# Attention with a bias on one NeuronCore: groups that go on with the last chunks, places filled as they come free, and a rearranged start

## The chip, the cores and the metric

The kernel runs on one core of a Trainium2 chip. A core has five engines that run side by side and wait for one another through semaphores: TensorE (PE; its weight loads are listed apart as PEld), VectorE (DVE), ScalarE (ACT), GpSimd (POOL) and SyncE (SP). SP, ACT and POOL also issue DMA transfers. The metric is the device time of one execution in microseconds; lower is better. The time before is 250.87 us, the median of three runs (250.59 to 251.34).

## The reference

Four batches of eight heads, 1024 positions, head size 64, all float32; the bias is one 1024 x 1024 matrix for all heads:

```python
scores = scale * np.matmul(q, k.transpose(0, 1, 3, 2))     # scale = 1/8
scores = scores + bias
scores_max = np.max(scores, axis=-1, keepdims=True)
attn = np.exp(scores - scores_max) / (np.sum(np.exp(scores - scores_max), axis=-1, keepdims=True) + 1e-8)
return np.matmul(attn, v).astype(np.float32)
```

The kernel works in bfloat16, leaves the maximum out (the values are small), and gets the sum of the exponentials from a column of ones beside v.

## The kernel before

**Slots.** The 32 heads are taken as 16 pairs; a pair's q and k lie side by side as 128 columns. The 1024 queries of a head are 8 chunks of 128. One chunk of one head is a slot, so there are 256 slots. A slot's scores (128 x 1024) are made in one of three *places* in PSUM (`places`), by 8 matmuls of 128 x 128 (`fill`, L210). ACT takes the exponential of a place in one instruction (`exp`, L217) and writes an E tile (9 buffers, `NE`). PE then multiplies E with v (`av`, L276, 8 matmuls) into a bank shared with the transposes (`ps_x`, two tags, xa and xb). When a batch of six slots is done, VectorE divides by the sums (`evac`, L284 and L287), and SP sends the rows out (L300).

**The bias is put into a place once.** The first fill of a place for a chunk adds the bias by 8 more matmuls against a scaled identity (L205). After that, the next head's fill goes on top: its operands hold the next head's product and, with the sign turned, the last head's, so that one matmul takes the old scores out and puts the new ones in. That is what the doubled operands are for: `ko`, `qo` for odd heads, `ke`, `qe` for even ones, where one half of `ke` and `qe` comes from the pair before (`double`, L183 and L185; part 1 writes into the next pair's arrays). A slot with a bias fill uses `qe` of the first pair, or `qs` of a pair in the middle, whose lower half is zero. `linked` says whether a pair's arrays go on into the next pair; it is false at the end of a group.

**Groups.** The pairs fall into three groups of 4, 6 and 6. Within a group the chunks go 0 to 2 for all heads (place x takes chunk x), then 3 to 5, and then 6 and 7, where the third place takes chunks 6 and 7 of the last third of the heads. Every group starts all of it anew, so there are 30 bias fills.

**VectorE does some exponentials.** 15 slots, spread evenly over batches (`dslots`), have no exponential on ACT: VectorE makes it in seven instructions (`d_steps`, L237 to L260), the first of which (`dy`) frees the place.

**Preparing q and k.** Each pair is loaded by POOL's DMA queue with a cast (L128, L129), copied side by side by VectorE (`side_by_side`, L135), transposed by PE (L165, 8 per piece), copied out of PSUM by VectorE (`copy_out`, L172 and L174), and doubled, on VectorE if it is wanted soon, else on POOL. v goes straight into its array (L146), or, for the first four pairs, through a landing tile and a VectorE copy (L414). Pair 0's q and k and the first bias row come as float32 by the queues of SP and ACT and are cast by VectorE and ACT (L305 to L341).

**The order of the work** is written out by a planner that runs when the kernel is built. It keeps a clock for each engine with assumed costs in ns (a fill 450, `AV` 255, an exponential 906, a ke copy 340), and emits at each step the instruction that can start first. Slots are filled strictly in their order (`next_fill`); transposes of a piece are emitted in one go. Each engine then runs its list in that order, and waits where an operand isn't ready.

Of the kernel before, what the change touches and what calls it, by code (L numbers as in the profile page):

```python
# [16 lines left out]
def kernel(  # L17
# [13 lines left out]
    nc = tc.nc  # L31
# [23 lines left out]
    qsp = ctx.enter_context(tc.tile_pool(name="qsp", bufs=1))  # L55
    ep = ctx.enter_context(tc.tile_pool(name="ep", bufs=NE))
    op = ctx.enter_context(tc.tile_pool(name="op", bufs=3))
# [10 lines left out]
    sgn = consts.tile([P, 1], F32)  # L68
    zeros = consts.tile([P, 512], BF)
# [3 lines left out]
    q0f = consts.tile([P, 2, NCH, D], F32)  # L73
# [3 lines left out]

    slots = []
    batches = []
    first_pair, split_pair = set(), set()  # L80
    group_of = {}
    pr0 = 0
    for g, n in enumerate(GROUPS):
        heads = list(range(2 * pr0, 2 * (pr0 + n)))
        for pr in range(pr0, pr0 + n):
            group_of[pr] = g
        first_pair.add(pr0)
        rounds = []
        for c in (0, 3):
            rounds += [[(x, c + x, h, h == heads[0]) for x in range(3)] for h in heads]  # L90
        a = (len(heads) * 2 // 3 + 1) // 2 * 2
        tail = [(2, c, h, h == heads[a]) for c in (6, 7) for h in heads[a:]]
        split_pair.add(heads[a] // 2)
        for i, h in enumerate(heads[:a]):
            rounds.append([(0, 6, h, h == heads[0]), (1, 7, h, h == heads[0])] + tail[i:i + 1])
        assert len(tail) <= a
        for i in range(0, len(rounds), 2):
            b = []
            for r in rounds[i:i + 2]:
                b += range(len(slots), len(slots) + len(r))  # L100
                slots += r
            batches.append(b)
        pr0 += n
    NS, NB = len(slots), len(batches)
# [14 lines left out]
    can = [b for b in range(2, NB - 3) if len(batches[b]) == 6]  # L119
    ND = 15  # L120
    dslots = [batches[can[(2 * i + 1) * len(can) // (2 * ND)]][5] for i in range(ND)]
    aslots = [s for s in range(NS) if s not in dslots]
# [3 lines left out]
    def load_qk(pr):  # L126
        f = [land.tile([P, 2, NCH, D], BF, name=x) for x in ("q16", "k16")]
        nc.gpsimd.dma_start(out=f[1].rearrange("p t c d -> p t (c d)"), in_=kf[pr])  # L128
        nc.gpsimd.dma_start(out=f[0].rearrange("p t c d -> p t (c d)"), in_=qf[pr])  # L129
        lands[pr] = f  # L130

    def side_by_side(pr, x):

        t = raw.tile([P, NCH, 2, D], BF, name="qk"[x] + "r")
        nc.vector.tensor_copy(t.rearrange("p c t d -> p t c d"), lands[pr][x][:])  # L135
        raws[pr, x] = t
# [11 lines left out]
    def arrays(pr):  # L148
        if pr not in arrs:
            t = {x: kq.tile([P, NCH, P], BF, name=x) for x in ("ko", "ke", "qo", "qe")}  # L150
            if pr in split_pair:
                t["qs"] = qsp.tile([P, NCH, P], BF, name="qs")
                nc.gpsimd.memset(t["qs"][D:, :, :], 0.0)
            if pr in first_pair:
                (nc.gpsimd if pr else nc.vector).memset(t["qe"][D:, :, :], 0.0)
            arrs[pr] = t
        return arrs[pr]

    def linked(pr):
        return pr + 1 < NP and pr + 1 not in first_pair  # L160

    def transposes(pr, which, c0, n, tag):
        px = ps_x.tile([P, n, P], BF, tag=tag, name="px")
        for c in range(n):
            nc.tensor.transpose(px[:, c, :], raws[pr, which][:, c0 + c].rearrange("p t d -> p (t d)"), ident[:])  # L165
        return px
# [9 lines left out]
    def double(pr, which, c0, n, part, w):  # L176
# [7 lines left out]
        else:  # L184
            w.tensor_scalar(to["qs" if part == 2 else "qe"][rows, cs, :], t["qo"][rows, cs, :], -1.0, 1.0,  # L185
                            op0=ALU.mult, op1=ALU.mult)

    def parts(pr, which):
        return ([0] if not which or pr not in first_pair else []) + ([1] if linked(pr) else []) + (
            [2] if not which and pr in split_pair else [])  # L190

    def operands(s):
# [3 lines left out]
        if start:  # L196
            return t["ko"], t["qe"] if pr in first_pair else t["qs"]
        return (t["ko"], t["qo"]) if h % 2 else (t["ke"], t["qe"])

    def fill(s):  # L200
        x, c, h, start = slots[s]
        ps = places[x]
        if start:
            for kc in range(NCH):
                nc.tensor.matmul(ps[:, kc // 4, kc % 4 * P:(kc % 4 + 1) * P],  # L205
                                 braw[:, c, :].rearrange("p (kp kc) -> p kc kp", kc=NCH)[:, kc, :], ident8[:],
                                 start=kc % 4 == 0, stop=False, skip_group_check=True)
        kk, qq = operands(s)
        for kc in range(NCH):
            nc.tensor.matmul(ps[:, kc // 4, kc % 4 * P:(kc % 4 + 1) * P], kk[:, kc, :], qq[:, c, :],  # L210
                             start=False, stop=True, skip_group_check=True)
# [3 lines left out]
    def exp(s):  # L215
        etile[s] = ep.tile([P, NCH, P], BF, name="E")
        nc.scalar.activation(etile[s].rearrange("p c q -> p (c q)"), places[slots[s][0]].rearrange("p b x -> p (b x)"),  # L217
                             ACTF.Exp, scale=scale)
# [60 lines left out]
    def evac(b):  # L279
# [7 lines left out]
        nc.vector.tensor_tensor(ob[:, :m, :], po[:, :m, :D], rs[:, :m, :].to_broadcast([P, m, D]), op=ALU.mult)  # L287
# [15 lines left out]
    with tc.manual_schedule():  # L303

        nc.sync.dma_start(out=k0f[:, 0].rearrange("p c d -> p (c d)"), in_=kf[0][:, 0])  # L305
        nc.scalar.dma_start(out=q0f[:, :, :C0].rearrange("p t c d -> p t (c d)"), in_=qf[0][:, :, :C0 * D])
        nc.sync.dma_start(out=k0f[:, 1].rearrange("p c d -> p (c d)"), in_=kf[0][:, 1])
        nc.scalar.dma_start(out=b0f[:], in_=bf_[:, 0, :])
        nc.sync.dma_start(out=q0f[:, :, C0:].rearrange("p t c d -> p t (c d)"), in_=qf[0][:, :, C0 * D:])
# [6 lines left out]
        nc.gpsimd.dma_start(out=braw[:, 1, :], in_=bf_[:, 1, :])  # L316
        nc.gpsimd.dma_start(out=braw[:, 2, :], in_=bf_[:, 2, :])
        load_qk(1)
        for i in range(10):
            nc.tensor.matmul(places[2][:, 0, :], zeros[:, :P], zeros[:], start=True, stop=True)  # L320
        qr0 = raws[0, 0] = raw.tile([P, NCH, 2, D], BF, name="qr")
        kr0 = raws[0, 1] = raw.tile([P, NCH, 2, D], BF, name="kr")
        t0 = arrays(0)
        nc.vector.memset(vall[:, :, :, D:D1], 1.0)
        nc.vector.tensor_scalar(ident8[:], ident[:], 1.0 / scale, None, op0=ALU.mult)
        load_v(0)
        load_qk(2)
        load_v(1)
        load_qk(3)
        load_v(2)  # L330
        nc.vector.tensor_copy(qr0[:, :C0].rearrange("p c t d -> p t c d"), q0f[:, :, :C0])
        nc.vector.tensor_copy(kr0[:, :, 0, :], k0f[:, 0])
        nc.vector.tensor_copy(kr0[:, :, 1, :], k0f[:, 1])
        nc.scalar.copy(braw[:, 0, :], b0f[:])  # L334
        pq = transposes(0, 0, 0, C0, "xa")
        for i in range(2):
            nc.tensor.matmul(places[2][:, 0, :], zeros[:, :P], zeros[:], start=True, stop=True)
        copy_out(0, 0, 0, C0, pq)
        nc.vector.tensor_copy(t0["qe"][:D, :C0, :], pq[:D])
        copy_out(0, 1, 0, NCH, transposes(0, 1, 0, NCH, "xb"))  # L340
# [357 lines left out]
```

## Time and profile before

| | |
|---|---|
| median of three runs | 250.87 us |
| profiled execution, its time | 251.34 us |
| its span | 249.57 us |
| exponentials on ACT | 241 (224.0 us busy) |
| first exponential starts, last one ends | 10.69 us, 244.16 us |
| seventh exponential (the first of pair 1) starts | 17.87 us |
| VectorE busy | 203.0 us |
| PE busy | 227.8 us |
| bias fills | 30 (240 matmuls of L205) |

The span begins with the first instruction of the program and ends with its last. "Busy" is the time in which an engine has at least one instruction running; instructions overlap at their ends, so the mean duration of one may be more than busy time over their number. PE clock stays at full speed from 4.7 us to the end of the work. The page names a wait by what ended it.

### The profile page before, as it was taken

Reading aid. Unit: us, or ns where it says so; the run is one execution under the profiler, and the core shown is the slowest. Engines: PE = TensorE matmul, PEld = TensorE weight load, DVE = VectorE, ACT = ScalarE, POOL = GpSimd, SP = SyncE. Lnnn points to the kernel's source line nnn. Section 1 sums busy time; section 2 is a strip of 40 time slices with the busy share of each in tenths; the row PEclk is TensorE's granted clock in tenths of the full one; section 3 lists DMA queues with packets and bytes.
Section 4 is the critical chain, followed back from the end, with each engine's and each line's share of the span. In section 5 each row is a group of like instructions: output and inputs, shape, how many; then the busy total and the mean of one; then the engine's idle time right before and its main releaser. Section 6 shows DMA issues by size and latency. Waiting matters only on the chain.

```text
span 249.6 us, 10411 instructions
## 1 busy us (share of the span) xinstructions
PE 227.8 (91%) x4604; PEld 216.3 (87%) x4604; DVE 203.0 (81%) x334; ACT 226.5 (91%) x244; POOL 69.5 (28%) x86
## 2 busy tenths in 40 slices
PE   8579999999999989998897999898999999999981
PEld 3469999899999989998897999898999998899970
DVE  5389788897969999999999999999999773977111
ACT  2479999999997999999998999899999999999991
POOL 8335986171461413535740002300000000000000
PEclk9999999999999999999999999999999999999997
DMA  6999999996987699799592021101111111111121
GB/s 214 223 205 209 207 206 189 202 128 92 139 131 61 105 123 133 123 129 131 96 96 67 3 68 37 34 24 51 43 53 34 39 58 30 41 34 46 29 65 33
DMA packets 53229, 24.53 MB, mean 98 GB/s; under 512 B 31680, under 2 KB 51904, under 8 KB 53184
## 3 DMA queue, kind: packets, MB, share of 16 engines
q0 software_dynamic: 35216, 13.90, 47.8%
q1 hardware_dynamic: 17552, 9.25, 13.3%
q8 instruction: 36, 0.59, 1.0%
q10 hardware_dynamic: 416, 0.72, 0.9%
q14 instruction: 9, 0.07, 0.1%
HBM read 29.36 MB, written 8.39 MB: 151 GB/s over the span
## 4 chain that ended last, share of the span: by engine, by line
PE 47%; DVE 23%; ACT 12%; issue 11%; DMA 4%; ACTq 1%; SPq 0%; DVEq 0%
PE pl L210 26%; PE po L276 13%; ACT E L217 11%; PE pl L205 6%; DVE dy L237 3%; DMA b0f<-in_bias_dram 3%; PE px L165 3%; DVE ob L287 3%; DVE ke L183 2%; DVE qo L174 2%; DVE ko L172 1%; DVE qe L185 1%; DVE de L260 1%; DVE dpw L246 1%; DVE rs L284 1%
## 5 line engine op out<-in xcount | busy, mean ns | idle before, releaser
L217 ACT ACTIVATE E<-pl 128x1024 bf16<-128x1024 f32 x241 | 224.0, 1079 | 10.7 <-PE pl L210 8.5
L276 PE MATMUL po<-vall,E 128*128 128x65 bf16 x1928 | 93.9, 194 | 3.4 <-DVE qo L174 1.9
L276 PEld LDWEIGHTS <-E 128*128 128x128 bf16 x1928 | 79.3, 98 | 4.6 <-issue 2.4
L210 PEld LDWEIGHTS <-ko 128*128 128x128 bf16 x1264 | 75.8, 98 | 3.3 <-issue 0.7
L210 PE MATMUL pl<-qo,ko 128*128 128x128 bf16 x1024 | 76.3, 219 | 1.3 <-issue 0.6
L210 PE MATMUL pl<-qe,ke 128*128 128x128 bf16 x784 | 58.5, 219 | 4.6 <-DVE dy L237 3.2
L210 PEld LDWEIGHTS <-ke 128*128 128x128 bf16 x784 | 47.1, 98 | 7.7 <-issue 4.2
L284 DVE RECIPROCAL rs<-po 128x6 f32<-128x6 f32 (+2 forms) x43 | 8.3, 193 | 23.4 <-PE po L276 23.1
L287 DVE TENSOR_TENSOR ob<-po,rs 128x384 f32<-128x384 f32 (+2 forms) x43 | 22.9, 531 | 1.8 <-DVE rs L284 0.3
L205 PE MATMUL pl<-ident,braw 128*128 128x128 bf16 x240 | 19.9, 226 | 4.1 <-ACT braw L334 3.0
L146 POOL DMA_DIRECT2D vall<-in_v_dram x24 | 22.3, 934 | 1.4 <-DMA vall<-in_v_dram 1.2
L205 PEld LDWEIGHTS <-braw 128*128 128x128 bf16 x240 | 18.1, 148 | 4.7 <-ACT braw L334 3.2
L237 DVE TENSOR_SCALAR dy<-pl 128x1024 int32<-128x1024 f32 x15 | 18.3, 1220 | 3.7 <-PE pl L210 3.3
L185 POOL TENSOR_SCALAR qe<-qo 64x1024 bf16<-64x1024 bf16 (+1 forms) x10 | 12.6, 1261 | 30.5 <-DVE qo L174 30.0
L128 POOL DMA_DIRECT2D k<-in_k_dram x15 | 11.0, 731 | 36.1 <-DVE kr L135 32.5
L249 DVE SCALAR_TENSOR_TENSOR dy<-df 128x1024 f32<-128x1024 f32 x15 | 19.0, 1269 | 0.3
L256 DVE SCALAR_TENSOR_TENSOR db<-db,dpw 128x1024 f32<-128x1024 f32 x15 | 18.3, 1221 | 0.3
L260 DVE SCALAR_TENSOR_TENSOR de<-dy,db 128x1024 bf16<-128x1024 f32 x15 | 18.3, 1220 | 0.2
L249 DVE SCALAR_TENSOR_TENSOR db<-df 128x1024 f32<-128x1024 f32 x15 | 18.2, 1217 | 0.0
L183 DVE COPY ke<-ko 64x1024 bf16<-64x1024 bf16 x26 | 15.4, 594 | 0.7
L129 POOL DMA_DIRECT2D q<-in_q_dram x15 | 11.5, 768 | 12.7 <-DVE qr L135 11.0
L210 PE MATMUL pl<-qe,ko 128*128 128x128 bf16 x192 | 14.6, 219 | 0.0
(49 smaller groups left out, 149.2 us busy)
## 6 DMA issues: line engine op xcount, KB each, us to landing
out_dram<-ob SPq DMA_DIRECT2D x52, 96.0 KB, 2.7
k<-in_k_dram POOLq DMA_DIRECT2D x15, 256.0 KB, 4.9
q<-in_q_dram POOLq DMA_DIRECT2D x15, 256.0 KB, 7.2
vall<-in_v_dram POOLq DMA_DIRECT2D x24, 128.0 KB, 6.7
out_dram<-ob SPq DMA_DIRECT2D x34, 64.0 KB, 1.7
braw<-in_bias_dram POOLq DMA_DIRECT2D x7, 256.0 KB, 7.8
v<-in_v_dram POOLq DMA_DIRECT2D x4, 256.0 KB, 8.1
out_dram<-ob SPq DMA_DIRECT2D x17, 32.0 KB, 1.6
```

The lines of the kernel that those rows point to most:

```text
L146: nc.gpsimd.dma_start(out=vall[:, 2 * pr + t, :, :D], in_=vf[pr, :, t])
L183: w.tensor_copy(to["ke"][rows, cs, :], t["ko"][rows, cs, :])
L185: w.tensor_scalar(to["qs" if part == 2 else "qe"][rows, cs, :], t["qo"][rows, cs, :], -1.0, 1.0, op0=ALU.mult, op1=ALU.mult)
L205: nc.tensor.matmul(ps[:, kc // 4, kc % 4 * P:(kc % 4 + 1) * P], braw[:, c, :].rearrange("p (kp kc) -> p kc kp", kc=NCH)[:, kc, :], ident8[ ...
L210: nc.tensor.matmul(ps[:, kc // 4, kc % 4 * P:(kc % 4 + 1) * P], kk[:, kc, :], qq[:, c, :], start=False, stop=True, skip_group_check=True)
L217: nc.scalar.activation(etile[s].rearrange("p c q -> p (c q)"), places[slots[s][0]].rearrange("p b x -> p (b x)"), ACTF.Exp, scale=scale)
L237: w.tensor_scalar(y[:], places[slots[s][0]].rearrange("p b x -> p (b x)"), scale * LOG2E * 65536.0, 127.0 * 65536.0, op0=ALU.mult, op1=ALU ...
L249: w.scalar_tensor_tensor(o[:], t["f"][:], c, t["f"][:], op0=ALU.add, op1=ALU.mult)
L256: w.scalar_tensor_tensor(t["b"][:], t["b"][:], V2, t["p"].bitcast(BF), op0=ALU.add, op1=ALU.mult)
L260: w.scalar_tensor_tensor(etile[s].rearrange("p c q -> p (c q)"), t["a"], V1, t["b"][:], op0=ALU.add, op1=ALU.mult)
L276: nc.tensor.matmul(po[:, j, :], etile[s][:, kc, :], vall[:, h, kc, :], start=j == 0 and kc == 0, stop=kc == NCH - 1, skip_group_check=True)
L287: nc.vector.tensor_tensor(ob[:, :m, :], po[:, :m, :D], rs[:, :m, :].to_broadcast([P, m, D]), op=ALU.mult)
```

## The change

- *Groups go on with the last chunks.* A group's chunks are now three stretches: three chunks at one end, chunks 3 and 4 in the middle (third place: chunks 3 and 4 of the last third of the heads), and three chunks at the other end. Odd groups run from chunk 5 down to 0, so that a group begins with the chunks with which the one before ended and needs no new bias there. `linked` now holds for all pairs but the last. Bias fills: 24. The last round's three slots are a batch of their own.
- *Places filled in order of release.* Each place has its own queue of slots, and the planner may fill any place whose next slot is at most 4 (`WINDOW`) beyond the oldest open one. Which slots VectorE takes is decided while planning: a slot of place 2 goes to VectorE if its backlog is under 5000 ns (`ROOM`). There are 16 of them.
- *Half transposes.* A piece's transposes are emitted in two halves, other work may stand between them, and they are held back while E tiles pile up.
- *q of first pairs in two parts.* Pairs 0 to 3 load, copy, transpose and double chunks 0 to 2 of q first, and the other five later, in POOL's queue behind the first loads.
- *First slot by banks.* The first slot's k is handled in halves (one cast on ACT), and its bias, scores and exponential are made bank by bank, so that ACT has two half exponentials there.
- *b0 first.* ACT's queue loads the first bias row before anything else; SP's queue loads pair 0's first q chunks and k in two halves.
- The zeroed operands `qs` and `qz` (which takes the part that `qe` of a group's first pair had) are now constants, two of them set by POOL ahead of its loads. Output tiles have two buffers instead of three. Two of twelve idle matmuls at the start are gone.

```diff
-    op = ctx.enter_context(tc.tile_pool(name="op", bufs=3))
+    op = ctx.enter_context(tc.tile_pool(name="op", bufs=2))
...
-        for c in (0, 3):
-            rounds += [[(x, c + x, h, h == heads[0]) for x in range(3)] for h in heads]
         a = (len(heads) * 2 // 3 + 1) // 2 * 2
-        tail = [(2, c, h, h == heads[a]) for c in (6, 7) for h in heads[a:]]
+        tail = [(2, c, h, h == heads[a]) for c in (3, 4) for h in heads[a:]]
+        middle = [[(0, 3, h, h == heads[0]), (1, 4, h, h == heads[0])] + tail[i:i + 1] for i, h in enumerate(heads[:a])]
+        ends = [[[(x, c + x, h, h == heads[0] and (go or g == 0)) for x in range(3)] for h in heads]
+                for go, c in enumerate((5, 0) if g % 2 else (0, 5))]
+        rounds = ends[0] + middle + ends[1]
...
+    last = [s for s in batches[-1] if s >= len(slots) - len(rounds[-1])]
+    batches[-1] = batches[-1][:-len(last)]
+    batches.append(last)
...
-    ND = 15
-    dslots = [batches[can[(2 * i + 1) * len(can) // (2 * ND)]][5] for i in range(ND)]
+    dslots = set()
+    may_d = [x[0] == 2 and 24 < s < NS - 12 and not any(y[3] for y in slots[s:s + 4]) for s, x in enumerate(slots)]
...
     def linked(pr):
-        return pr + 1 < NP and pr + 1 not in first_pair
+        return pr + 1 < NP
...
+        n = 1 if s == 0 else 2
+        for i in range(0, 2, n):
+            nc.scalar.activation(e[:, i:i + n].rearrange("p b x -> p (b x)"),
+                                 places[slots[s][0]][:, i:i + n].rearrange("p b x -> p (b x)"), ACTF.Exp, scale=scale)
...
+        nc.sync.dma_start(out=q0f[:], in_=qf[0][:, :, :C0 * D].rearrange("p t (c d) -> p t c d", d=D))
         nc.scalar.dma_start(out=b0f[:], in_=bf_[:, 0, :])
...
+        nc.gpsimd.memset(qz[0][D:, :, :], 0.0)
+        nc.gpsimd.memset(qs[D:, :, :], 0.0)
+        first, rest = slice(0, C0), slice(C0, NCH)
+        for c in (1, 2):
+            nc.gpsimd.dma_start(out=braw[:, c, :], in_=bf_[:, c, :])
+        load_k(1)
+        load_q(1, first)
+        load_v(0)
+        load_k(2)
+        load_q(2, first)
...
+        nc.scalar.copy(braw[:, 0, :], b0f[:])
+        nc.scalar.copy(kr0[1][:, :half].rearrange("p c t d -> p t c d"), k0f[:, :, half:])
+        pq = transposes(0, 0, 0, C0, "xa")
+        pk = transposes(0, 1, 0, half, "xb")
+        nc.vector.tensor_scalar(t0["qz"][:D, :C0, :], pq[:D], 1.0, None, op0=ALU.mult)
+        copy_out(0, 1, 0, half, pk)
+        copy_out(0, 0, 0, C0, pq)
+        for i in range(2):
+            fill_half(0, i, "b")
+        fill_half(0, 0, "s")
+        copy_out(0, 1, half, half, transposes(0, 1, half, half, "xb"))
+        fill_half(0, 1, "s")
...
-            if next_fill < NS:
-                s = next_fill
+            for x in range(3):
+                if not queue[x] or queue[x][0] > next_fill + WINDOW:
+                    continue
+                s = queue[x][0]
...
+                        if may_d[s] and backlog(t) < ROOM:
+                            dslots.add(s)
+                            avq.remove(s)
                             start_d(s)
...
+                if ((pr, which, c0) in raw_at and next_fill >= need - AHEAD and (ring < 0 or last_slot[ring] < next_fill)
+                        and (lag < 6 or need - next_fill < 8 or half_done)):
```

## The prediction

> **What bounds the kernel now.** First the page: busy shares and the rows of 40 slices (each digit tenths of 6.24 us).
>
> ```profile
> span 249.6 us, 10411 instructions
> PE 227.8 (91%) x4604; PEld 216.3 (87%) x4604; DVE 203.0 (81%) x334; ACT 226.5 (91%) x244; POOL 69.5 (28%) x86
> DVE  5389788897969999999999999999999773977111
> ACT  2479999999997999999998999899999999999991
> ```
>
> ACT is the engine that never rests, and VectorE (DVE) stands at nine tenths from slice 13 to 31. A share alone doesn't say which waits end last, so next the busy time by stage (us; from the first exponential, from the seventh, through VectorE's full stretch, to the last).
>
> ```profile
> 10.69:17.87 7.18, 5.58 (x97) 5.21 (x96) 5.21 (x12) 5.64 (x6) 2.33 (x4) 1.00 1.24 205
> 17.87:78.70 60.83, 58.95 (x1215) 57.12 (x1213) 51.51 (x87) 58.91 (x64) 32.89 (x40) 1.00 1.22 161
> 78.70:176.20 97.50, 90.92 (x1923) 88.49 (x1921) 95.08 (x152) 91.83 (x99) 27.31 (x28) 1.00 0.55 79
> 176.20:244.16 67.96, 65.47 (x1336) 61.86 (x1332) 45.89 (x70) 67.63 (x74) 0.00 (x0) 1.00 0.16 43
> ```
>
> The columns are PE, weight loads, DVE, ACT, POOL, then clock, DMA share and GB/s. ACT's idle time is length minus busy: 1.54 in the first row, then 1.92, 5.67 and 0.33: 7.92 after the seventh exponential. In the third row VectorE works 95.08 of 97.50; there it is the bound and ACT follows. The last row has 22 us of VectorE idle. Then the costliest groups and two waits.
>
> ```profile
> L217 ACT ACTIVATE E<-pl 128x1024 bf16<-128x1024 f32 x241 | 224.0, 1079 | 10.7 <-PE pl L210 8.5
> L183 DVE COPY ke<-ko 64x1024 bf16<-64x1024 bf16 x26 | 15.4, 594 | 0.7
> ACT E L217 <- PE pl L210: 8.5, 14, 1.5
> PE pl L210 <- DVE dy L237: 3.2, 3, 1.4
> ```
>
> One exponential takes 224.0/241 = 0.93 us of ACT (they overlap, so not 1.079). ACT waits for fills; 3.2 us of what fills wait for is a place that VectorE's own exponential (dy) holds. Last the time line of the head and the end.
>
> ```profile
> 8.40 1.04 ACT L334 CAST braw<-b0f 128x1024 bf16<-128x1024 f32 x1 [5.14 <-DMA b0f<-in_bias_dram]
> 10.69 5.64 ACT L217 ACTIVATE E<-pl 128x1024 bf16<-128x1024 f32 x6 [1.25 <-PE pl L210]
> 11.86 0.43 DVE L135 COPY kr<-k 128x1024 bf16<-128x1024 bf16 x1 [0.62 <-DMA k<-in_k_dram]
> 13.18 0.43 DVE L135 COPY qr<-q 128x1024 bf16<-128x1024 bf16 x1 [0.89 <-DMA q<-in_q_dram]
> 17.22 1.51 PE L210 MATMUL pl<-qe,ke 128*128 128x128 bf16 x24
> 17.87 11.22 ACT L217 ACTIVATE E<-pl 128x1024 bf16<-128x1024 f32 x12 [1.54 <-PE pl L210]
> ...
> 244.91 0.56 DVE L287 TENSOR_TENSOR ob<-po,rs 128x384 f32<-128x384 f32 x1
> 245.50 1.76 SPq L300 DMA_DIRECT2D out_dram<-ob  x4
> ```
>
> The seventh exponential, pair 1's first, waits for pair 1's q (landed 13.15). The span is 17.87, 235 exponentials at 0.93 with 7.9 of gaps, and 5.4 after the last one ends (244.16).
>
> **The sum is made against the profiled execution**, 251.34 us (span 249.57 and 1.77 around it), 0.47 above the median of the three runs, 250.87; a result is brought to the median by taking 0.47 off. No change can be told within about 0.3%, 0.75 us.
>
> **Part 1, the head (q of the first pairs in two parts, b0 first, first slot by banks, constants on POOL).** SP and ACT queues load 256+256+192+512+320 = 1536 KB before, 192+512+512 = 1216 KB after (the rest of q0 moves to POOL's queue, behind bias row 3). At the 317 GB/s of 4.0 to 6.5 us the 320 KB are 1.0 us. On POOL's queue two memsets (qs and qe rows: 0.97 each) now stand ahead of every load: each is issued 1.94 later. Those loads moved no packet until 5.6, though the first was issued at 1.43, since the other queues had the engines; so the delay costs between 0 and 1.94. I take 0.7, nearer to 0 since 5.6 was not set by the issue. Then k1 lands at 11.84-1.0+0.7 = 11.6. q1's first part is 96 KB in place of 256; 160 KB at 205 GB/s are 0.8, so it lands at 13.15-1.0-0.8+0.7 = 12.1. From there, by the rows: kr copy 0.43, 8 transposes 0.6, ko 0.69, ke 0.42, qo 0.40 (128x384), ke 0.42, two qe at 0.26, a fill 0.5 and its latency: 11.6 to about 15.5. The old way took 17.87. The six exponentials of pair 0 must be done by then. b0f now leads ACT's queue, 0.5 earlier and without 192 KB (0.6) ahead, and the HWDGE bytes thin out: it lands at 6 to 7.3 rather than 8.37. Cast 1.04, the k half's cast on ACT 0.56 (as L332), 4 transposes, ko half 0.4, half a fill: the first half exponential near 9, its second half behind one more copy; six end at 14.6 to 15.4. Hidden then. Two half exponentials in place of one add at most one exponential's latency, 0.15, inside this. The gain is 2.4; ends: 2.9 (POOL's delay nothing) and 0 (delay whole, and bias rows late).
>
> A rule to weigh: two loads that followed each other on POOL's queue fed copies at 11.86 and 13.18, 1.32 apart, which is 256 KB at 205 GB/s with nothing added per transfer. [...]
>
> **Part 2, one exponential fewer on ACT.** The built order has 16 on VectorE, not 15; ACT does 240: -0.93. VectorE pays 1.220+0.690+0.771+1.269+1.217+1.221+1.220 = 7.6 and 0.21 for its own output row. That is in part 3.
>
> **Part 3, the body.** Bias fills drop from 30 to 24 (8 matmuls each, 0.49): 2.9 us less of PE, and where three stood in a row ACT idled 0.2 to 0.6. VectorE gains work: 30 ke copies, not 26 (linked pairs across groups), and pieces of q halves that POOL did (10 down to 5 on POOL). What it takes is counted from the built order, from the 5th to the 33rd evacuation (28 of them) with before's means: db 22x1.219, de 11x1.220, dy 11x1.269 and 12x1.220, df 11x0.690, dpw 11x0.771, ke 23x0.594, ko 12x0.685, kr 11x0.459, qr 11x0.449, qe/qs/qz 22x0.452, qo 12x0.745, ob 16x0.558+11x0.491+0.425, od 10x0.214, rs 28x0.192: 157.8. The same count of before's third row gives 101.4 for 97.50 of time (overlap), so 157.8x0.962 = 151.8. ACT does 154 exponentials in between, 143.1. VectorE lacks 8.7. Some is taken up: the backlog can grow. Before, ACT was 1 exponential ahead of what the evacuation at 68.1 needed, 6 ahead at 176.2; five are 4.6. So ACT loses 4.1 here. From the 33rd on VectorE needs less than ACT (61 instructions, some 44 us against 52), so nothing. Outside I take 1.5: two bias clusters at about 0.5, 0.3 at the end and a little. Gaps 5.6 against 7.9: -2.3. Ends: 1.5 (ke at its 0.42 minimum takes 3.9 off, the backlog the rest) and 12 (nothing absorbed, and q pieces late, 2). The filling by order of release, the half transposes (same 256 matmuls) and one output buffer fewer (op: 2; landings of 1.6 to 2.7 median against two evacuations, some 10 us) I cost at nothing: PE has 8 to 10% of idle time and ACT decides. Without that cover a row of late transposes is 0.6 and one late output buffer up to 2.
>
> **Part 4, the end.** The last batch is one head's three chunks and one VectorE row: +0.25 PE, ob about 0.36 (64 columns are 0.067 by the rows 0.558, 0.491, 0.425) and od 0.21 for 0.56; two issues, not four, so the last starts 0.38 after the first rather than 1.32: -0.6 (ends -0.9 and +0.5, if the last VectorE exponential is late).
>
> **Sum:** -2.4 -0.9 -2.3 -0.6 = -6.2; 251.34-6.2 = 245.1; at the median 244.7.
>
> **Rivals.**
> - *VectorE takes back more.* Its rows speak for it (95.08 of 97.50), and the full stretch now begins 35 us earlier. Backlog absorbs nothing: gaps 8.7+1.5 = 10.2, +4.6: 249.3. Against: it did absorb before. 0.13, of which 0.03 within the bound.
> - *Slower: VectorE's order is written for other durations.* The planner counts 340 ns for a ke copy (row 594) and 590 for ko (685), about 3.2 us a pair against 4.4, and q of a group's pairs is now made closer to its use: pair 9's q stands behind the 15th evacuation, about four slots ahead. In the first passes of groups 1 and 2, 12 pairs fall behind by 1.2 each; less the 4.6 of backlog that is 10 more: 254. It decides once gaps pass 12.5. Against: before's planner had the same durations and lost 1.36 there. 0.11.
> - *Everything absorbed.* ke copies were long only beside POOL's work (0.42 median, 1.44 longest), which shrinks: gaps 2, 241.1. 0.11.
> - *The head doesn't move.* POOL's 1.94 in full and bias rows late: no 2.4, 247.1. 0.08.
> - *Each transfer pays a time of its own.* If each of the four added transfers takes as long as a whole 256 KB one (1.32), the last q rest lands 5 us later, near 31, with 2 us of VectorE work to follow, and chunk 3 wants it at 32: 1 lost, 245.7. The copies at 11.86 and 13.18 speak against it. 0.02. [...]
>
> **Chances.** Forecast 0.55. Faster 0.55+0.10+0.11+0.08+0.02, less 0.01 for ends of the forecast that reach the bound = 0.85; same 0.04; slower 0.11. The range runs from the absorbed case, 240.8, to the first rival, 249.8.
>
> **What would show it.** In the changed profile: pair 1's first exponential near 15.5 (head right), not 17; 240 exponentials; ACT's gaps after it near 5.6, mostly between 40 and 190 us, with VectorE above 0.97 busy there; 4.8 between the last exponential and the end. Wrong if fills wait for qe or dy by over 8 us in all, if ke copies average over 0.7, or if VectorE's last exponential ends after ACT's.

## The result, and the profile after

The changed kernel takes 247.0 us (median of 4 runs, 246.85 to 247.3) against 250.84 for the kernel before on the same chip: a ratio of 0.9846, with a 95% interval from 0.9828 to 0.9864. It is 1.5% faster; the forecast was 244.7 with a range from 240.8 to 249.8. The profiled execution after has a span of 245.5 us and a time of 247.3, so 4.04 less than the one before in both, of the 6.2 forecast.

First the page of the changed kernel: busy times, the rows of slices for VectorE and ACT, and the two costliest groups that answer to those shown before.

```profile
span 245.5 us, 10300 instructions
PE 223.2 (91%) x4554; PEld 211.3 (86%) x4554; DVE 214.5 (87%) x370; ACT 226.7 (92%) x245; POOL 61.9 (25%) x82
DVE  3669963989999999999999999999999999499991
ACT  3689999999999989999999998999999999999991
L237 ACT ACTIVATE E<-pl 128x1024 bf16<-128x1024 f32 (+1 forms) x241 | 223.6, 1072 | 9.1 <-PE pl L223 8.1
L195 DVE COPY ke<-ko 64x1024 bf16<-64x1024 bf16 x30 | 14.5, 484 | 0.8
```

The 241 instructions are 240 exponentials, the first of them in two halves. VectorE's row of nines now begins at slice 10 and not at 13. Then the busy time by stage, cut at the seventh exponential, VectorE's 5th and 33rd evacuation, and the end of the last exponential (columns as in the prediction: PE, weight loads, DVE, ACT, POOL, clock, DMA share, GB/s).

```profile
15.93:42.50 26.57, 25.56 (x542) 24.86 (x540) 18.40 (x49) 25.63 (x28) 17.71 (x25) 1.00 1.36 197
42.50:192.10 149.60, 140.52 (x2942) 135.53 (x2939) 144.74 (x235) 144.40 (x156) 33.54 (x38) 1.00 0.66 90
192.10:240.11 48.01, 44.59 (x942) 42.50 (x939) 42.34 (x62) 47.86 (x52) 0.00 (x0) 1.00 0.16 43
240.11:245.53 5.42, 0.95 (x24) 0.82 (x24) 0.67 (x3) 0.00 (x0) 0.00 (x0) 0.65 0.14 42
```

ACT is idle for 0.94, 5.20 and 0.15 us in the first three rows, 6.29 in all after the seventh exponential (7.92 before). The terms of the sum, span against span (249.57 and 245.53):

| term | before | after | change | forecast |
|---|---|---|---|---|
| start of the 7th exponential | 17.87 | 15.93 | -1.94 | -2.4 |
| ACT busy from there on | 218.37 | 217.89 | -0.48 | -0.93 |
| ACT's gaps from there on | 7.92 | 6.29 | -1.63 | -2.3 |
| behind the last exponential | 5.41 | 5.42 | +0.01 | -0.6 |

How a gap of the body comes about can be read on the time line of the changed kernel (start, length, engine, line; in brackets the idle time before and what ended it):

```profile
72.33 0.56 DVE L308 TENSOR_TENSOR ob<-po,rs 128x384 f32<-128x384 f32 x1
72.94 0.43 PE L296 MATMUL po<-vall,E 128*128 128x65 bf16 x8 [0.75 <-DVE ob L308]
...
76.16 1.22 DVE L257 TENSOR_SCALAR dy<-pl 128x1024 int32<-128x1024 f32 x1
76.42 1.94 ACT L237 ACTIVATE E<-pl 128x1024 bf16<-128x1024 f32 x2 [0.52 <-PE pl L223]
77.44 0.27 PE L223 MATMUL pl<-qe,ke 128*128 128x128 bf16 x2 [0.35 <-DVE dy L257]
```

PE's written order has products with v next, and these want a PSUM bank that VectorE's evacuation (ob) empties late. PE stands for 0.75 us, the fills behind it are late, and ACT is short of a fill 3.5 us later. That the one wait led to the other is read from the order; the rows alone don't show it.

### The profile page after: what moved, and what is told of

It is laid out like the page before. It is cut to its first block, busy times and chain, and to the rows that moved or that the text cites. A ratio compares the mean times of both kernels' runs of the same rounds, so it can differ in the third digit from the quotient of the medians.

```text
span 245.5 us, 10300 instructions
## 1 busy us (share of the span) xinstructions
PE 223.2 (91%) x4554; PEld 211.3 (86%) x4554; DVE 214.5 (87%) x370; ACT 226.7 (92%) x245; POOL 61.9 (25%) x82
## 4 chain that ended last, share of the span: by engine, by line
DVE 41%; PE 29%; ACT 17%; issue 9%; DMA 2%; ACTq 0%; SPq 0%; DVEq 0%
PE pl L223 17%; ACT E L237 17%; PE po L296 7%; DVE qo L186 4%; DVE dy L257 4%; DVE ke L195 4%; DVE ob L308 4%; DVE qe L197 3%; DVE de L280 3%; DVE ko L184 3%; PE pl L220 3%; DVE db L276 3%; DVE dy L269 3%; DVE db L269 2%; DMA k0f<-in_k_dram 2%
## 5 line engine op out<-in xcount | busy, mean ns | idle before, releaser
L237 ACT ACTIVATE E<-pl 128x1024 bf16<-128x1024 f32 (+1 forms) x241 | 223.6, 1072 | 9.1 <-PE pl L223 8.1
L296 PE MATMUL po<-vall,E 128*128 128x65 bf16 x1920 | 89.1, 194 | 6.1 <-DVE ob L308 2.2
L223 PEld LDWEIGHTS <-ko 128*128 128x128 bf16 x1216 | 72.4, 98 | 6.6 <-issue 4.6
L223 PE MATMUL pl<-qe,ke 128*128 128x128 bf16 x832 | 62.3, 219 | 4.0 <-DVE qe L197 1.8
L308 DVE TENSOR_TENSOR ob<-po,rs 128x384 f32<-128x384 f32 (+3 forms) x44 | 22.9, 521 | 1.8 <-DVE rs L304 0.3
L257 DVE TENSOR_SCALAR dy<-pl 128x1024 int32<-128x1024 f32 x16 | 19.5, 1220 | 4.7 <-ACT E L237 3.5
L220 PE MATMUL pl<-ident,braw 128*128 128x128 bf16 x192 | 16.0, 226 | 0.1
L184 DVE COPY ko<-px 128x1024 bf16<-128x1024 bf16 (+1 forms) x17 | 11.1, 651 | 4.2 <-PE px L177 4.2
L186 DVE TENSOR_SCALAR qo<-px,sgn 128x1024 bf16<-128x1024 bf16 (+2 forms) x20 | 12.7, 637 | 2.2 <-PE px L177 2.0
L197 DVE TENSOR_SCALAR qe<-qo 64x1024 bf16<-64x1024 bf16 (+2 forms) x33 | 13.4, 407 | 0.9
L304 DVE RECIPROCAL rs<-po 128x5 f32<-128x5 f32 (+4 forms) x44 | 8.4, 192 | 6.5 <-PE po L296 6.2
```

The source lines that it names most:

```text
L186: nc.vector.tensor_scalar(t["qo"][:, cs, :], px[:], sgn[:], None, op0=ALU.mult)
L220: nc.tensor.matmul(to, braw[:, c, :].rearrange("p (kp kc) -> p kc kp", kc=NCH)[:, kc, :], ident8[:], start=i == 0, stop=False, skip_group_ ...
L223: nc.tensor.matmul(to, kk[:, kc, :], qq[:, c, :], start=False, stop=True, skip_group_check=True)
L237: nc.scalar.activation(e[:, i:i + n].rearrange("p b x -> p (b x)"), places[slots[s][0]][:, i:i + n].rearrange("p b x -> p (b x)"), ACTF.Ex ...
L257: w.tensor_scalar(y[:], places[slots[s][0]].rearrange("p b x -> p (b x)"), scale * LOG2E * 65536.0, 127.0 * 65536.0, op0=ALU.mult, op1=ALU ...
L296: nc.tensor.matmul(po[:, j, :], etile[s][:, kc, :], vall[:, h, kc, :], start=j == 0 and kc == 0, stop=kc == NCH - 1, skip_group_check=True)
```

## The experiments

The measure used below beside the time is the *excess*: the distance of one exponential's start from the next, less 0.906 us (what the planner counts for one), summed from the seventh to the last. It is 13.0 before and 11.8 after. It doesn't go down to nothing: the run without VectorE's slots below, with 1.27 us of idle time on ACT, still has 4.4. "Slots of VectorE" are the exponentials that VectorE makes. The experiments ran in three sets, each beside the kernel before on the same chip: 251.13 us (the first two below, strict order, thirty bias fills), 250.96 (the planner's durations, the end, transposes in one go, clearings on VectorE) and 251.09 (the other four). Ratios are against these; differences in us are between medians of the sets and the changed kernel's 247.0.

### Is VectorE's amount of work the bound of the body?

**Two slots fewer for VectorE.**

```diff
+    may_d = [s in [35, 51, 54, 105, 108, 120, 132, 144, 159, 192, 204, 225, 228, 240] for s in range(NS)]
-        ROOM = 5000
+        ROOM = 1e9
```

> The changed kernel with 14 slots on VectorE instead of 16 (the same set without slots 75 and 180, which stand in the first passes of groups 1 and 2). Theory V: the gaps of ACT between 42 and 192 us (5.2 us) come from VectorE's total work there. Two exponentials off it are 15.6 us less of its work and 1.86 us more for ACT; the gaps there shrink to about 1.5 and the time falls by 1.8, to 245.2. Rival O: the gaps come from the order written for PE and would be there with an idle VectorE; they stay, and the time rises by 1.86, to 248.9.

Measured: 247.22 us (ratio 0.9837, 0.9784 to 0.9891), excess 12.0. Two exponentials more on ACT (1.86 us) and no fewer gaps; the time is held only because the end became 4.0 instead of 5.4 and the seventh exponential came 0.34 sooner. The same stretch as above:

```profile
42.50:192.10 149.60, 139.30 (x2921) 134.70 (x2919) 136.81 (x225) 144.48 (x156) 34.02 (x38) 1.00 0.66 90
```

VectorE works 7.9 us less in it (136.81 against 144.74) and ACT is idle just as long: 5.12 against 5.20. So over this step the gaps don't follow the amount of VectorE's work. Theory V had expected them to shrink to about 1.5; rival O had the gaps right and the time 1.7 too high, since it left the head and the end as they were.

**No slot for VectorE.** All 256 exponentials are on ACT.

```diff
+    may_d = [s in [] for s in range(NS)]
-        ROOM = 5000
+        ROOM = 1e9
```

> The changed kernel with all 256 exponentials on ACT. ACT has 16 more, 14.9 us. Theory V: all gaps after the seventh exponential fall from 6.3 to 2 or less, so 247.0+14.9-4.5 = 257.4 or below. Rival O: the gaps stay, 261.9.

Measured: 252.5 us (1.0056, 1.003 to 1.0082).

```profile
42.50:192.10 149.60, 142.51 (x2893) 134.96 (x2891) 60.40 (x129) 149.26 (x164) 49.71 (x55) 1.00 0.65 90
```

In the same stretch ACT is idle for 0.34 us instead of 5.20, and from 49.50 to 246.70 for 0.01, so nearly all gaps of the body come with VectorE's slots. Exponentials without a gap between them take 0.917 us (197.19 over 215), 0.931 in the changed kernel; this, the end (4.0) and the head bring the time well below the 257.4 that theory V gave as its upper end. Sixteen slots take 16 x 0.93 = 14.9 us off ACT and the kernel gains 5.5 by them.

**The planner's durations.** The planner counts 340 ns for a ke copy (row 484), 590 for ko (651), 1140 for dy (1220). Here its prices are set near the rows, or a little above: for the seven steps of an exponential, the copies side by side and the doubles (`60 + 35 * n`), v's copies (not shown), the copies out of PSUM, and the evacuations. It then gives VectorE 14 slots.

```diff
-        return [(1140, fixed), (610, frac), (720, power), (1145, lambda: quad(t["a"], U1)), (1145, quad2),
-                (1250, scaled), (1145, last)]
+        return [(1240, fixed), (710, frac), (790, power), (1240, lambda: quad(t["a"], U1)), (1240, quad2),
+                (1240, scaled), (1240, last)]
...
-            cost = 60 + 35 * n
+            cost = 110 + 42 * n
...
-                                done = t2 + 60 * n + 110
+                                done = t2 + 66 * n + 200
...
-            cost = 225 + 67 * m + 75 + (len(units) - m) * 130
+            cost = 225 + 67 * m + 125 + (len(units) - m) * 215
```

> The changed kernel with the planner's VectorE durations set to the rows of the profile (ke 340 to 446, ko 590 to 728, dy 1140 to 1240 and so on); its backlog limit then gives VectorE 14 slots, as in the run with two fewer. Theory L: VectorE is late because the order is written for shorter durations; with the right ones PE stands less, the excess over back-to-back exponentials falls from 12.0 (the run with two fewer) to about 8, and the time to 243.5. Rival: a bank waits whenever 1.2 us steps of VectorE's exponentials stand in its list, whatever was planned; as with two fewer, 247.2.

Measured: 245.95 us (0.9799, 0.9754 to 0.9844), excess 8.3. The excess is what the theory of late steps had, with its 14 slots against the 14 of the first experiment: 12.0 there, 8.3 here, and 1.98 us of idle time on ACT from 42.50 to 192.10 instead of 5.12. The time misses that theory's 243.5, and its interval overlaps the changed kernel's. Its head is worse than the changed kernel's: the seventh exponential starts at 16.97 and not at 15.93, since other prices write another head too.

**The end.** No slot for VectorE among the last 24 (15 slots).

```diff
-    may_d = [x[0] == 2 and 24 < s < NS - 12 and not any(y[3] for y in slots[s:s + 4]) for s, x in enumerate(slots)]
+    may_d = [x[0] == 2 and 24 < s < NS - 24 and not any(y[3] for y in slots[s:s + 4]) for s, x in enumerate(slots)]
```

> The changed kernel without a VectorE exponential in the last 24 slots (15 instead of 16; slot 240 goes to ACT). The last batch then has no row of VectorE's behind it. Theory: the end after the last exponential, 5.4 us now, falls to 4.0 as in the run with two fewer; ACT has 0.93 more and some 0.5 of gaps less: 246.0. Rival: the end is noise of the landing and stays 5.4: 247.4 to 247.9.

Measured: 246.86 us (0.9828, 0.9784 to 0.9871). The end falls from 5.4 to 3.9, as the theory said; one more exponential (0.93) stands against it, and the gaps of the body are those of the changed kernel (5.21 against 5.20), so the time lies between the two expectations.

**Durations behind the head, and the end.** The prices above apply once 20 slots are filled, the last 24 slots are kept from VectorE, and the backlog limit is 6500 ns, since backlog is now counted in longer prices. It has 14 slots.

```diff
-        ROOM = 5000
+        ROOM = 6500
-            cost = 60 + 35 * n
+            cost = 110 + 42 * n if next_fill > 20 else 60 + 35 * n
...
-    may_d = [x[0] == 2 and 24 < s < NS - 12 and not any(y[3] for y in slots[s:s + 4]) for s, x in enumerate(slots)]
+    may_d = [x[0] == 2 and 24 < s < NS - 24 and not any(y[3] for y in slots[s:s + 4]) for s, x in enumerate(slots)]
```

> The changed kernel with the planner's durations from the rows only once 20 slots are filled (so the head is written as in the changed kernel), no slot for VectorE among the last 24, and a backlog limit of 6500 ns for the longer prices; 14 exponentials on VectorE. The theory that the gaps of the body come from an order of VectorE written for too short durations: the head is back (7th exponential at 15.9 instead of 17.0 of the run with the durations everywhere, about -1.0), the end is 3.9 instead of 5.4 (-1.5), the body as in that run: 245.95 - 1.0 - 1.5 = 243.4 us (243.0 to 244.2). The rival, that the body is bound by VectorE's work whatever the order and the earlier run won by a lucky place of its 14: gaps of 5 us in the body again, 245.0 to 247.0.

Measured: 241.58 us (6 runs, 241.24 to 242.71), ratio 0.9629 (0.9604 to 0.9654): 5.4 us below the changed kernel's 247.0, 1.8 below the theory's 243.4, and the fastest of all. Excess 5.6. The stages, cut as before:

```profile
span 239.4 us, 10293 instructions
15.62:42.50 26.88, 25.88 (x549) 25.16 (x547) 17.99 (x50) 25.94 (x28) 18.17 (x25) 1.00 1.36 198
42.50:192.10 149.60, 145.09 (x3046) 140.62 (x3044) 140.68 (x223) 148.49 (x162) 47.80 (x46) 1.00 0.67 92
192.10:235.44 43.34, 40.14 (x840) 38.19 (x837) 34.17 (x50) 43.34 (x48) 0.00 (x0) 1.00 0.16 44
235.44:239.40 3.96, 0.69 (x16) 0.57 (x16) 0.54 (x2) 0.00 (x0) 0.00 (x0) 0.93 0.14 43
```

In the middle stretch VectorE is busier than in the first experiment (140.68 against 136.81), with 14 slots in both kernels, and ACT is idle for 1.11 us instead of 5.12. Between these two the order decides, not the amount. Against the run with the durations everywhere the span is 4.5 shorter: 1.35 in the head, 2.45 between the seventh and the last exponential, 0.7 at the end. The 2.45 was expected to be nothing; which of the edits (limit, later prices, the last 24) brings it wasn't separated. Nor was the order of the steps separated from the places of the slots: no run gave the changed kernel's own slots the new prices. The three runs with new prices (this one, the one before it and the next) have three different sets of slots and 1.1 to 2.0 us of idle time in the stretch, which speaks against one lucky set.

**GpSimd copies nothing.** As the kernel just above, with all halves doubled on VectorE (13 slots).

```diff
-                if which or urgent:
+                if True:
```

> As the run before it, and GpSimd copies no half of q: all doubles go to VectorE (13 exponentials on VectorE then, so one more on ScalarE, +0.93 us). If VectorE's steps beside GpSimd's copies (kr 1.2 to 1.3 instead of 0.42, db and dy 1.9 to 2.05 instead of 1.22) are what leaves the last gaps of the body, 1.5 to 2 us of gaps go and the time is 0.5 to 1 us below the run before: 242.5 to 243.2. If those steps are hidden by the backlog, it is one exponential slower: 244.0 to 244.6.

Measured: 242.51 us (0.9653, 0.9631 to 0.9674), 0.93 above the run before it, which is the price of the one exponential more; the two intervals overlap. It lies in the first theory's numbers only because the run before it came out 1.8 below its own forecast. Excess 5.8, and ACT's idle time in the stretch is 1.33 against 1.11. VectorE's steps beside GpSimd's copies are longer (kr 1.21 and 1.26 us in the changed kernel, 0.42 in the median), but taking the copies away wins nothing; that the backlog hides them is argued, not shown. GpSimd's 13 copies in the kernel above (5 in the changed one) are not what makes it fast either.

### What the parts of the change are worth

**Places filled in strict order.**

```diff
-        WINDOW = 4
+        WINDOW = 0
-        ROOM = 5000
+        ROOM = 4500
```

> The changed kernel with places filled strictly in the order of slots (window 0; the backlog limit 4500 instead of 5000 keeps 16 slots on VectorE). If VectorE's work sets the body, the order of the fills moves little: 247.0 to 247.7, with more waits of fills for VectorE's dy (2.0 now, 3.2 before the change). Rival: filling in order of release is what carries the body's gain, and the 1.6 us that the gaps lost come back or more: 248.6 to 250.

Measured: 248.33 us (0.9878, 0.9824 to 0.9932), 1.3 above the changed kernel, with an interval that overlaps its own: between the two expectations. In the profiled execution the body is clearly worse, excess 15.4, and the end is 4.0 instead of 5.4, which hides part of that. The stretch as above, with 8.96 us of idle time on ACT, and two windows behind the head:

```profile
42.50:192.10 149.60, 138.62 (x2895) 133.57 (x2892) 143.94 (x231) 140.64 (x152) 39.50 (x43) 1.00 0.66 90
12.84:16.25 3.41, 1.40 (x26) 1.28 (x24) 3.19 (x9) 2.45 (x3) 0.29 (x1) 1.00 1.31 201
16.25:19.67 3.42, 3.42 (x40) 3.42 (x38) 2.12 (x4) 2.23 (x3) 3.09 (x5) 0.50 1.25 199
```

The last row shows the granted clock at 0.50 for 3.42 us after PE had waited 2.01 us for qe. This is not what the 1.3 consist of: the profiled execution (249.49) has a mean clock of 0.988, the other three (247.95 to 248.43) one of 0.995 to 0.999.

**All thirty bias fills**, with the slots of VectorE held fixed.

```diff
-        ends = [[[(x, c + x, h, h == heads[0] and (go or g == 0)) for x in range(3)] for h in heads]
+        ends = [[[(x, c + x, h, h == heads[0]) for x in range(3)] for h in heads]
```

> The changed kernel with a bias fill again at the start of groups 1 and 2 (30 bias fills, the same 16 slots on VectorE, all else kept; for the scores they are the same sums made anew). Theory V: PE has room, and two clusters of three bias fills cost ACT 0.3 to 0.5 each: 247.6 to 248.0. Rival P: PE's time counts in full, 48 matmuls and weight loads of bias, 2.9 us: 249.9.

Measured: 249.12 us (0.9913, 0.9885 to 0.9941), 2.1 above the changed kernel and between the two expectations. ACT is idle for 8.11 us after the seventh exponential (6.29), with a gap of 1.51 us some 7 us behind the first added set of fills (65.7 to 69.3) and four of 0.6 to 1.0 besides. PE is busy for 2.3 us more (225.5 against 223.2).

**Transposes of a piece in one go**, with the slots held fixed.

```diff
-                    to = n if half_done else (n + 1) // 2
-                    cost = (n // 2 if half_done else to) * 56
+                    to = n
+                    cost = 0 if half_done else to * 56
```

> The changed kernel with each piece's transposes emitted in one go (16 slots on VectorE, the same ones). Theory L: PE, in its written order, stands at products and transposes that wait for a bank which VectorE empties late; the size of a transpose block is not what it waits for, so 247.0 to 247.5. Rival H: blocks of 0.49 us instead of 0.25 push fills back at many of the 32 pieces, 0.1 to 0.25 each: 248.5 to 250.

Measured: 250.52 us (0.9972, 0.9949 to 0.9994), 3.5 above the changed kernel, excess 14.6. The rival was right, or still low. One place on this kernel's time line shows how late steps add up, and the windows behind it what follows; what the longer blocks themselves did can't be singled out there.

```profile
147.70 1.26 DVE L150 COPY kr<-k 128x1024 bf16<-128x1024 bf16 x1
148.89 0.67 DVE L186 COPY ko<-px 128x1024 bf16<-128x1024 bf16 x1
149.61 0.31 PEld L298 LDWEIGHTS <-E 128*128 128x128 bf16 x8 [2.33 <-DVE ko L186]
```

```profile
147.60:151.00 3.40, 1.38 (x32) 1.39 (x33) 3.30 (x7) 2.31 (x4) 1.08 (x1) 1.00 0.11 31
151.00:154.41 3.41, 3.41 (x44) 3.41 (x42) 3.11 (x4) 2.54 (x3) 0.81 (x1) 0.50 0.17 53
```

PE's weight loads stood 2.33 us for the bank that ko empties, and then PE had half its clock for 3.41 us. The clock is the smaller part of the loss: the one execution of ten with a mean clock of 0.997 took 249.80, the other nine, at 0.983 to 0.991, from 249.92 to 251.10.

**The two clearings on VectorE**, so that GpSimd's loads are issued at once. The order of each engine is otherwise unchanged.

```diff
-        nc.gpsimd.memset(qz[0][D:, :, :], 0.0)
-        nc.gpsimd.memset(qs[D:, :, :], 0.0)
+        nc.vector.memset(qz[0][D:, :, :], 0.0)
+        nc.vector.memset(qs[D:, :, :], 0.0)
```

> The changed kernel with the two memsets that stand ahead of POOL's loads done by VectorE (idle then). Theory: the seventh exponential waits for VectorE's copies behind PE's order (k1's transposes stand behind four fills and start at 12.35, though its copy is ready at 10.83), not for loads: it stays at 15.5 to 15.9 and the time at 247.0. Rival: POOL's delay of 1.9 us counts, the first loads land 1 to 1.9 earlier, and with them the seventh exponential: 245.1 to 246.0.

Measured: 250.75 us (0.9996, 0.9972 to 1.0019), 3.7 above the changed kernel: nearly the whole gain is gone, which neither expectation allowed for. The loads are issued 1.7 us earlier (1.44 instead of 3.17), but the first of them lands at 7.80 instead of 7.87. What it shares the DMA engines with (busy share 1.04 from 4.0 to 6.5 us) is late: the second half of k0 lands at 9.49 instead of 6.77. On this kernel's time line, and in its windows:

```profile
9.51 0.62 ACT L365 CAST kr<-k0f 128x512 bf16<-128x512 f32 x1 [3.23 <-DMA k0f<-in_k_dram]
10.19 0.61 PE L177 MATMUL px<-ident,kr 128*128 128x128 bf16 x4 [2.29 <-ACT kr L365]
```

```profile
6.22:9.63 3.41, 1.45 (x18) 0.99 (x16) 1.31 (x4) 0.18 (x2) 1.46 (x3) 1.00 1.14 227
9.63:13.04 3.41, 2.33 (x21) 2.08 (x22) 1.80 (x5) 1.58 (x3) 1.95 (x3) 0.50 1.29 202
13.04:16.45 3.41, 3.41 (x35) 3.41 (x33) 0.00 (x0) 2.17 (x4) 0.00 (x0) 0.50 1.30 199
```

2.72 us of a late transfer become 4.28 of a late start (the seventh exponential at 20.21, not 15.93), since the clock is at 0.50 for 6.82 us. This execution (251.69) is one of the three longest of ten, with a mean clock of 0.984. The other seven, 250.25 to 250.80, have 0.987 to 0.989, where 6.82 us at 0.50 alone would bring it to an estimated 0.986 (3.41 lost of 250); so they spent less than that at it.

**The clearings twice**, which issues GpSimd's loads another 1.83 us later.

```diff
         nc.gpsimd.memset(qs[D:, :, :], 0.0)
+        nc.gpsimd.memset(qz[0][D:, :, :], 0.0)
+        nc.gpsimd.memset(qs[D:, :, :], 0.0)
```

> The changed kernel with the two clearings on GpSimd ahead of its loads done twice: its loads are issued about 1.9 us later, nothing else moves. The theory that the delay pays because the loads of GpSimd's queue and the first k, q and b0 share the DMA engines, and that it pays only as long as k is on its way: k's halves land as before (6.1 and 6.8, or 0.3 sooner), the second bias about 1.5 later (9.4), k1 at 12.0, the 7th exponential at 17.2 to 17.7: 248.3 to 249.0 us. The rival, that the transfers catch up (as they landed no sooner when they were issued 1.7 earlier): 246.7 to 247.5.

Measured: 247.71 us (0.9861, 0.9838 to 0.9883), an interval that overlaps the changed kernel's. k1 lands at 11.84, 1.46 later than in the changed kernel, as the theory said, and yet the seventh exponential starts at 16.01 against 15.93. Both expectations missed the reason. In the changed kernel k1's transposes stand behind four fills in PE's order and run at 12.35 only, though the copy kr is ready at 10.83: the load has 1.5 us of slack.

**Two clearings in the kernel before**, ahead of GpSimd's loads, of a tile that nothing reads.

```diff
+        for i in range(2):
+            nc.gpsimd.memset(pad[D:, :, :], 0.0)
         nc.gpsimd.dma_start(out=braw[:, 1, :], in_=bf_[:, 1, :])
```

> The kernel before with two such clearings (of a tile that nothing reads) on GpSimd ahead of its loads, 1.9 us of delay; nothing else moves. The theory that the delay pays by the DMA engines that it leaves to the first loads: b0 lands at 7.0 to 7.5 instead of 8.37, the first exponential comes 0.8 to 1.3 sooner, the second bias and k1 land within 0.5 of before: 249.5 to 250.5 us. The rival, that a delay ahead of the loads costs what it delays (the reading of the prediction): the 7th exponential 1 to 1.9 later, 251.9 to 252.8.

Measured: 250.81 us (0.9985, 0.997 to 1.0001), no change that can be told. b0 lands at 7.20 instead of 8.37, as the theory said; the loads issued 1.86 later land 0.3 to 0.4 earlier (the first bias row at 8.90 instead of 9.23, k1 at 11.49 instead of 11.84). But the first exponential comes only 0.43 sooner (10.26 against 10.69) and the seventh 0.38 later (18.25 against 17.87), as the clock drops to 0.50 here:

```profile
5.03:8.44 3.41, 1.72 (x17) 0.94 (x16) 2.26 (x6) 1.04 (x1) 3.41 (x6) 1.00 1.07 292
8.44:11.85 3.41, 3.41 (x34) 3.41 (x35) 1.11 (x3) 1.02 (x1) 1.79 (x3) 0.50 1.20 203
```

The delay is no cost in that kernel either; in the profiled execution (251.41) what it gave was lost again. Six of the ten executions have a mean clock of 0.995 to 0.997 (0.989 in the profiled one), too high for such a fall (3.41 us at 0.50 alone would make it an estimated 0.993); they took 250.29 to 251.00.

## Why the prediction was right and where it was wrong

The direction and the range held; 2.3 us of the forecast's size did not come. The time is that of the rival "The head doesn't move" (247.1), but not for its reason, since the head gained 1.94. The signs named beforehand came out (fills waited 1.8 us for qe and 2.0 for dy, ke copies took 0.484 in the mean), but they couldn't tell the forecast from the mechanism below.

**Part 1, the head: right in size, wrong in two steps.** The transfers came better than forecast: b0 landed at 5.27 (6 to 7.3 forecast), k1 at 10.38 (11.6; the sum written there gives 11.5), q1's first part at 10.93 (12.1). The step "From there, by the rows ... 11.6 to about 15.5" failed: a chain of durations, 3.9 long, took 5.55; 1.52 of it is that PE's written order puts k1's transposes behind four fills. So the loads weren't on the path at all within 1.5 us, and that the start came out so close (15.93 against 15.5) is luck: the two errors nearly cancel. The other failed step is the bound "the delay costs between 0 and 1.94" (the loads were issued 1.74 later). It left out a gain: without the delay the kernel is 3.7 us slower, though twice the delay gains no more. The prediction had seen that these loads "moved no packet until 5.6, though the first was issued at 1.43, since the other queues had the engines", and drew from it only that they lose nothing by waiting. It did not ask what the other queues lose to them.

**The four added transfers: no cost.** The three q rests and q0's rest (the five later chunks of pairs 0 to 3) stood with nothing in the sum. The last of them landed at 25.55 us, where the rival "Each transfer pays a time of its own" had it near 31, and the first fill of chunk 3 began at 32.1. The first 256 KB loads of the queue landed at 7.87, 9.11 and 10.38, so 1.24 and 1.27 apart, where 256 KB at the 204 GB/s of 6.5 to 9.4 us are 1.29: in a row, no time beside the bytes shows. What a transfer takes alone was not measured.

**Part 2, one exponential fewer: 0.48 and not 0.93.** Of the 0.93, 0.45 was lost in the mean length: 0.9292 us of busy time an exponential before, 0.9312 after.

**Part 3, the body: size nearly right by luck, mechanism wrong.** VectorE's stretch came out at 149.6 us (forecast 151.8) and the gaps at 6.29 (5.6). But the 151.8 was to be VectorE's work, and that came to 144.74, beside 144.40 of ACT's: VectorE lacked 0.3 and not 8.7, and with 4.6 of backlog the prediction's own step would have left no gap there. The step "VectorE lacks 8.7 ... the backlog can grow ... So ACT loses 4.1 here" is the one that failed. It takes the stretch to be bound by VectorE's amount of work. With 7.9 us of that work taken out ACT was idle as long as before; with the same 14 slots and another order it was idle for 1.11. A stretch in which an engine is 0.97 busy (144.74 of 149.60) is not shown to be bound by it; the gaps go with single late steps, for which PE stood in its written order. The rival "VectorE's order is written for other durations" had this mechanism. It gave it as a loss of 10 on top, to come only with a backlog that runs away; it is a loss of about 4 that was there all along (5.20 us of idle time in the stretch against 1.11), and most of the 6.1 us of span between the changed kernel and the fastest of the runs. Whether the durations alone undo it, or the places of the slots too, stays open.

**Costed at nothing.** The filling by order of release and the half transposes were costed at nothing, with PE's idle 8 to 10% as the cover. Undone, the half transposes cost 3.5 us and the order of release 3.8 of idle time in the stretch (8.96 against 5.20; in the time 1.3, not clear of the noise). So that cover isn't one. PE's idle time is made of waits in a written order and wasn't there to be spent; "a row of late transposes is 0.6" left out the clock, which was at 0.50 for 3.41 us behind a wait of 2.33 in the run with whole transposes.

**Part 4, the end: nothing and not 0.6.** The step "two issues, not four, so the last starts 0.38 after the first" held to the hundredth, and brought 0.94. Two other terms took it back. The last slots are filled out of order while products go in order, so two products and one of VectorE's follow the last exponential, and the first issue stands 1.77 us behind it, 1.34 before (0.26 of these 0.43 were forecast):

```profile
240.16 0.69 PE L296 MATMUL po<-vall,E 128*128 128x65 bf16 x16 [1.37 <-ACT E L237]
240.69 0.42 PE L296 MATMUL po<-vall,de 128*128 128x65 bf16 x8
241.15 0.18 DVE L304 RECIPROCAL rs<-po 128x4 f32<-128x4 f32 x1 [1.27 <-PE po L296]
241.37 0.36 DVE L308 TENSOR_TENSOR ob<-po,rs 128x192 f32<-128x192 f32 x1
241.64 0.21 DVE L312 TENSOR_TENSOR od<-po,rs 128x64 f32<-128x64 f32 x1
241.88 0.33 SPq L313 DMA_DIRECT2D out_dram<-od  x1
242.26 0.42 SPq L321 DMA_DIRECT2D out_dram<-ob  x1
```

And from the start of the last issue to the end of the span it took 3.27 us instead of 2.75, a term that the sum left as it was; what lengthens it is not shown. With no slot of VectorE near the end the whole is 3.9, below the forecast's 4.8.

## What to carry to other kernels

An engine that is 0.97 busy isn't thereby the bound: take some of its work out, and if the gaps stay, look at which of its steps come late in an order that was written for other durations. Where a planner writes the order, give it the durations that the profile's rows show; with that, a higher backlog limit and an end free of VectorE's long chains the kernel won another 5.4 us, where the whole change had won 3.8. Before a load is issued "as early as possible", ask which other transfer shares the DMA engines with it and who waits for that one.

## What the runs showed of the hardware

- *Loads on two queues held each other up.* GpSimd's loads issued 1.7 us sooner landed no sooner (7.80 against 7.87), and an SP load was 2.72 us later (9.49 against 6.77). In the kernel before, GpSimd's loads issued 1.86 us later landed 0.3 to 0.4 sooner, and b0, on ACT's queue, 1.17 sooner (7.20 against 8.37). How the engines divide their time between the queues is not shown.
- *TensorE's clock fell to half in the midst of the work.* In four profiles it was at 0.50 for 3.41 to 6.82 us, each time behind a stretch of 3.41 us in which PE had been busy for 1.38 (whole transposes), 1.40 (strict order), 1.45 (clearings on VectorE) and 1.72 us (two clearings in the kernel before); the rows stand with those runs. With the clearings on VectorE a stretch at half clock with 2.33 us of PE's work was followed by another at 0.50; behind the stretches at half clock in which PE was busy throughout, one in each of the four, the clock was at 1.00. The length of a wait alone doesn't tell whether the clock falls: it fell after PE had waited 2.01 us for qe (strict order), while in the kernel before PE stood for 3.00 us (6.50 to 9.50) and the clock stayed at 1.00. What decides it is not shown. The kernel before, around that wait:

```profile
4.71:8.12 3.41, 1.75 (x16) 0.84 (x14) 2.33 (x5) 0.00 (x0) 2.26 (x4) 1.00 1.03 285
8.12:11.53 3.41, 2.03 (x34) 2.04 (x35) 1.09 (x3) 1.88 (x2) 1.39 (x2) 1.00 1.19 212
```

Executions of one kernel differ in this: of the four with strict order, one alone has the low mean clock (0.988 against 0.995 to 0.999).
